# A two-layer attention, mLSTM and Mamba-2 encoder on one core: three token-stationary products at 512 columns, and a program order from an altered estimate

## The chip, the cores and the metric

The kernel runs on one core of one Trainium2 chip. The metric is device time in microseconds of one execution; before the change it is 1729.86 us (median of three runs, 1726.07 to 1732.43). The program is fixed: a Python layer writes out the instructions of every engine once, in one order, and the chip executes that order.

## The reference, cut to what matters

Two encoder layers run over 768 tokens of width 1024 (a request of 256 and one of 512), in float32. One layer is

```python
h = rms_norm(x, norm_g)
proj = h @ w_in                                   # 1024 -> 8224, all parts at once
ya = window_attention(rope(q), rope(k), v, sink) * silu(az)
yb = rms_norm(mlstm_bidir(mq, mk, mv, mi, mf)) * sigmoid(mo) * silu(mz)
yc = rms_norm(ssd_bidir(silu(conv(sxbc)), dt) * silu(sz))
merged = ga * (ya @ w_att_out) + gb * (yb @ w_mlstm_out) + gc * (yc @ w_ssm_out)
return x + merged @ w_out
```

where ga, gb and gc are sigmoids of further parts of proj.

## The kernel before, in words

**Products.** Every large product is computed in three parts: each float32 factor is split into a rounded high part and a remainder, both stored as float32r, and high*high, high*low and low*high are accumulated in PSUM. The activations lie split and transposed in the tile H. Weights come by DMA into a raw slot of 1024 words (`issue_raw`, line 591), ScalarE casts the high part, and VectorE or GpSimd subtracts it for the low part (`split_w`, 656). Split weights lie in one of four slots of 2048 words at the end of the tile R, or, for some pieces, in a block of R itself (`split_next`, 631).

**Items.** Each layer is a list of items (`ORDER`, line 20, built by `item_plan`). A "C" item (`item_C`, `mm_c`) keeps weights stationary and streams 512 and 256 tokens, so its output has channels on the partitions. A "T" item (`item_T`, 814, `mm_t`, 693) keeps 128 tokens stationary and streams the weights, so its output has tokens on the partitions: the queries (aq0, aq1), keys, values and gates (ak), the mLSTM values (mv0, mv1) and the SSD gate (sz0, sz1). aq, mv and sz are each two items of 256 columns. Per item and tile of 128 tokens that is 8 blocks of 128 rows times three parts, 24 matmuls. Weights of such an item are two pieces of 1024 words, dropped at the end of the item. "O", "P" and "W" items are the output products.

**Small work.** Norms, rotary embedding, attention, mLSTM and SSD are Python generators (`Task`, `Flow`, `mix_att`, `mix_mlstm`, `mix_ssd`, and the `..._put` functions behind each product). `tick` (557) is called between matmuls and writes the next steps of those generators whose inputs an estimate holds to be ready. `Clock.note` (238) keeps that estimate: when each engine is free and when each piece of memory was last written. `Watched.cost` (290) gives the duration of an instruction. The time "now" is the estimated time of TensorE. A transposition or a small matmul that a generator writes stands in TensorE's queue between the large matmuls; if its input is late on the chip, the large matmuls behind it wait too.

```python
t = max(t, (m[0][sl] + np.where(m[1][sl] != code, self.HOP, same)).max())
fin = t + cost
...
if ins[0].dtype == F32R:
    return max(53.0, n / 2.4)
```

All instructions are recorded through one helper, so the profile shows line 280 for each of them; they are told apart by tiles and shapes. "R,H" are the token-stationary products and the output product W, "H,R" the C items, "R" the products with the branch outputs, "F" the float32 transpositions and small matmuls.

**Memory.** The tile F holds 20096 words per partition, handed out and taken back by an `Arena` (102). Where there is no room, `alloc` raises an error while the program is written.

Of the kernel before, what the change touches and what calls it, by code (L numbers as in the profile page):

```python
# [55 lines left out]
def item_plan(layer):  # L56
# [4 lines left out]
    r0, r1, ra = range(0, 4), range(4, 8), range(0, 8)  # L61
# [15 lines left out]
    def one(word):  # L77
# [3 lines left out]
        elif name in ("aq", "mv", "sz"):  # L81
            t_item(name, idx, [({"aq": AQ, "mv": MV, "sz": SZ}[name] + 256 * idx, 256)])
# [101 lines left out]

INF = float("inf")


class Clock:
# [7 lines left out]
    def __init__(self):  # L196
        self.free = dict(pe=0.0, dve=0.0, act=0.0, pool=0.0, dma=0.0)
        self.mem = {}
        self.bank = [0.0] * 8
        self.psum = None  # L200
        self.last = 0.0

# [67 lines left out]
class Watched:  # L270
# [19 lines left out]
    def cost(self, name, out, ins, kw):  # L290
# [22 lines left out]
        if kw.get("op") == ALU.pow:  # L313
            return 300.0 + 164.0 * n
        return 150.0 + 2.1 * n
# [47 lines left out]
class Body:  # L363
    def __init__(self, tc, es, ins, outs):
# [44 lines left out]
        for l in range(NL):  # L409
            for kind, name, idx, pcs in item_plan(l):  # L410
# [10 lines left out]
                if name == "akv":  # L421
# [61 lines left out]
    def step(self, task, now):  # L483
# [11 lines left out]
        if isinstance(w, Task):  # L495
# [266 lines left out]
    def layer0_start(self):  # L762
# [16 lines left out]
        left = list(range(NT))  # L779
        for i in range(NT):  # L780
# [3 lines left out]
            if i < 2:  # L784
                self.issue_raw(1)
# [28 lines left out]
    def item_T(self, l, name, idx, ids):  # L814
# [10 lines left out]
        for i in ids:  # L825
            self.drop(i)

    def aq_begin(self, l, g):
        s = self.S[l]
        s["q", g] = self.R.alloc(4 * TOK)  # L830
        if g == 0:
            self.finish(s["consts"])
            s["k"] = self.R.alloc(4 * TOK)
            s["qkr"] = Ring(self.F, 5, 512)
            s["qks"] = Ring(self.F, 5, 8)

    def aq_epi(self, l, g, i, p):
        self.in_turn(self.S[l]["qkr"], lambda t: self.q_put(l, g, i, p, t))

    def qk_norm(self, l, i, p, nh, goff, t):  # L840
# [4 lines left out]
        t1, t2 = t[:, 0:n], t[:, 256:256 + n]  # L845
# [8 lines left out]
        self.rstd(st[:, 4:4 + nh], st[:, 0:nh], 1.0 / 64)  # L854
        yield
        nc.vector.tensor_tensor(out=a3, in0=a3, in1=st[:, 4:4 + nh].unsqueeze(2).to_broadcast([128, nh, 64]), op=ALU.mult)
# [12 lines left out]
    def q_put(self, l, g, i, p, t):  # L869
        nc = self.nc  # L870
        yield from self.qk_norm(l, i, p, 4, CB_QG, t)
        q4 = self.S[l]["q", g].ap.rearrange("p (j e t) -> p j e t", j=2, e=2)
        b, = yield 1
        for j in range(2):
            self.transpose_to(b[:, 128 * j:128 * j + 128], t[:, 128 * j:128 * j + 128])
        b3 = b[:, 0:256].rearrange("p (j t) -> p j t", j=2)
        ts = slice(128 * i, 128 * i + 128)
        half = [slice(0, 64), slice(64, 128)]
        for e in range(2):
            nc.scalar.copy(q4[half[e], :, e, ts], b3[half[e]])  # L880
        yield
        for e in range(2):
            nc.vector.tensor_tensor(out=q4[half[1 - e], :, e, ts], in0=b3[half[e]], in1=q4[half[e], :, e, ts].bitcast(F32),
                                    op=ALU.subtract)
        self.give(b)
        if i == NT - 1:
            self.flag(l, "qT", g)
# [15 lines left out]
    def k_put(self, l, i, p, t):  # L903
# [4 lines left out]
        nc.scalar.copy(t[:, 256:512].rearrange("p (v e d) -> p v e d", v=2, e=2),  # L908
                       t[:, 0:128].rearrange("p (v d) -> p v d", v=2).unsqueeze(2).to_broadcast([128, 2, 2, 64]))
        b, = yield 1  # L910
        for j in range(2):
            self.transpose_to(b[:, 128 * j:128 * j + 128], t[:, 256 + 128 * j:384 + 128 * j])
# [6 lines left out]
        if i == NT - 1:  # L919
            self.flag(l, "kT")  # L920

    def mv_begin(self, l, hp):
        s = self.S[l]
        b = s["mv", hp] = self.falloc(NT * 2 * 129)
        v = b.ap.rearrange("p (i h e) -> p i h e", i=NT, h=2)
        self.nc.gpsimd.memset(v[:, :, :, 128:129], 1.0)

    def mv_epi(self, l, hp, i, p):
        v = self.S[l]["mv", hp].ap.rearrange("p (i h e) -> p i h e", i=NT, h=2)
        self.nc.scalar.copy(v[:, i, :, 0:128], p.rearrange("p (h e) -> p h e", h=2))  # L930
        self.give(p)
        if i == NT - 1:
            self.flag(l, "mv", hp)

    def sz_begin(self, l, g):
        s, nc = self.S[l], self.nc
        if g == 0:
            s["szr"] = Ring(self.F, 3, 256)
            s["yc"] = self.R.alloc(8 * TOK)
            s["ycs"] = self.falloc(16)  # L940
            s["sng"] = self.falloc(512)
            s["ycr"] = Ring(self.F, 2, 512)
            s["ycn"] = NT

            def sng():
                nc.sync.dma_start(out=s["sng"].ap, in_=self.ins["cstb"][l:l + 1, CB_SNG:CB_ALL].to_broadcast([128, 512]))
                yield
                nc.gpsimd.tensor_scalar(out=s["sng"].ap, in0=s["sng"].ap, scalar1=0.5, scalar2=None, op0=ALU.mult)

            s["sngt"] = self.spawn(sng())  # L950
        else:
            self.finish(s["sngt"])
# [885 lines left out]
```

## Time and profile before

| | us |
|---|---|
| median of three runs | 1729.86 |
| the profiled execution | 1730.85 |
| its span | 1728.9 |
| TensorE busy | 1685.9 (98%) |
| VectorE busy | 938.6 (54%) |
| ScalarE busy | 643.5 (37%) |
| GpSimd busy | 382.8 (22%) |
| mean granted TensorE clock | 0.994 of full speed |

The span is from the first to the last instruction; the profiled execution took 1.95 us more than that. Busy times of matmuls overlap each other where they are pipelined, so durations of matmuls are best read from start to start.

### The profile page before, as it was taken

The page shows a single profiled execution, that of the slowest core. Times are in us where ns is not written, and L with a number is a line of the kernel's source. Part 1 is how long each engine was busy: PE and PEld are TensorE (multiplying, and loading weights), DVE is VectorE, ACT ScalarE, POOL GpSimd, SP SyncE. Part 2 cuts the span into 40 slices and gives each one's busy share as a digit, 9 for nine tenths or more (in the row PEclk, how much of TensorE's full clock was granted, in tenths as well). Part 3 has the DMA queues.
Part 4 walks back from the last instruction along what each step waited for, and adds up shares of the span by engine and source line. Part 5 has one row for each costly group of instructions (what it writes and reads, how often), then busy time and mean ns, then how long its engine had stood idle before and what let it go on. Part 6 is the DMA issues. An engine that isn't in the chain of part 4 may idle for free. (4 is left out here: it accounts for less than half of the span.)

```text
span 1728.9 us, 27389 instructions
## 1 busy us (share of the span) xinstructions
PE 1685.9 (98%) x10766; PEld 1487.3 (86%) x10766; DVE 938.6 (54%) x2176; ACT 643.5 (37%) x1461; POOL 382.8 (22%) x488
## 2 busy tenths in 40 slices
PE   8999999999999999999999999999999999999999
PEld 7888889988877878998798898898888878789987
DVE  6664556444577971256356544563445779613541
ACT  6446743322334421243143566432332244122320
POOL 6533310000113241014045333000001121400220
PEclk9999999999999999999999999999999999999999
DMA  4111122222114432145211101222121145222522
GB/s 175 63 50 38 38 95 77 79 77 71 57 51 140 168 111 90 56 155 168 97 62 39 62 25 50 83 77 89 67 71 59 61 147 189 99 75 68 183 85 74
DMA packets 47888, 152.29 MB, mean 88 GB/s; under 512 B 5616, under 2 KB 6544, under 8 KB 47760
## 3 DMA queue, kind: packets, MB, share of 16 engines
q1 hardware_dynamic: 47760, 150.55, 25.7%
q8 instruction: 85, 1.39, 0.3%
q14 instruction: 43, 0.35, 0.1%
HBM read 131.51 MB, written 19.02 MB: 87 GB/s over the span
## 5 line engine op out<-in xcount | busy, mean ns | idle before, releaser
L280 PE MATMUL psum<-H,R 128*128 128x512 f32 x4800 | 891.0, 341 | 0.1
L280 PEld LDWEIGHTS psum<-H,R 128*128 128x128 f32 x4800 | 734.9, 189 | 108.3 <-issue 8.9
L280 PE MATMUL psum<-R,H 128*128 128x256 f32 (+2 forms) x2616 | 397.5, 310 | 4.9 <-POOL R L280 3.1
L280 PEld LDWEIGHTS psum<-R,H 128*128 128x128 f32 x2616 | 360.4, 191 | 28.7 <-POOL R L280 3.3
L280 DVE TENSOR_TENSOR R<-F,R 128x1024 fp32r<-128x1024 f32 (+2 forms) x158 | 208.6, 1332 | 253.6 <-ACT R L280 253.5
L280 DVE SCALAR_TENSOR_TENSOR F<-F 128x128 f32<-128x128 f32 (+5 forms) x596 | 272.8, 504 | 59.8 <-POOL F L280 33.5
L280 PE MATMUL psum<-F 128*128 128x128 f32 (+7 forms) x2006 | 254.3, 289 | 34.9 <-DVE F L280 21.6
L280 POOL TENSOR_TENSOR F<-F 128x32 f32<-128x32 f32 (+8 forms) x276 | 226.9, 832 | 263.5 <-DVE F L280 222.8
L280 ACT ACTIVATE F<-F 128x128 f32<-128x128 f32 (+8 forms) x432 | 202.6, 496 | 185.8 <-DVE F L280 154.1
L280 PEld LDWEIGHTS psum<-F 128*128 128x128 f32 (+4 forms) x2006 | 203.0, 164 | 72.2 <-DVE F L280 29.5
L280 PE MATMUL psum<-R 128*128 128x512 f32 (+2 forms) x1344 | 249.8, 336 | 0.0
L280 ACT ACTIVATE F<-psum 128x768 f32<-128x768 f32 (+2 forms) x148 | 93.3, 630 | 397.0 <-PE psum L280 389.0
L280 POOL TENSOR_SCALAR F<-F 128x256 f32<-128x256 f32 (+7 forms) x124 | 78.8, 638 | 714.5 <-ACT F L280 521.3
L280 PEld LDWEIGHTS psum<-R 128*128 128x128 f32 x1344 | 204.3, 189 | 29.1 <-issue 3.0
L280 ACT CAST R<-F 128x1024 fp32r<-128x1024 f32 (+4 forms) x226 | 194.2, 876 | 70.5 <-DVE F L280 34.8
L280 ACT COPY F<-psum 128x256 f32<-128x256 f32 (+5 forms) x298 | 108.5, 392 | 207.6 <-PE psum L280 195.9
L280 DVE SCALAR_TENSOR_TENSOR F<-F,psum 128x768 f32<-128x768 f32 (+3 forms) x136 | 90.4, 674 | 109.6 <-ACT F L280 57.0
L280 POOL TENSOR_TENSOR R<-F,R 128x128 fp32r<-128x128 f32 (+2 forms) x68 | 76.3, 1124 | 246.0 <-ACT R L280 243.7
L280 DVE SCALAR_TENSOR_TENSOR F<-psum,F 128x128 f32<-128x128 f32 (+4 forms) x75 | 37.4, 505 | 161.1 <-PE psum L280 160.4
L280 DVE TENSOR_TENSOR F<-F 128x2 f32<-128x2 f32 (+8 forms) x376 | 102.6, 281 | 33.3 <-POOL F L280 16.5
L280 DVE TENSOR_SCALAR F<-F 128x128 f32<-128x128 f32 (+5 forms) x230 | 64.7, 309 | 49.7 <-ACT F L280 25.7
L280 DVE TENSOR_TENSOR F<-F,psum 128x129 f32<-128x129 f32 (+2 forms) x104 | 36.0, 376 | 39.2 <-ACT F L280 21.0
(24 smaller groups left out, 280.0 us busy)
## 6 DMA issues: line engine op xcount, KB each, us to landing
F<-wts_dram SPq DMA_DIRECT2D x164, 512.0 KB, 3.5
mg<-F SPq DMA_DIRECT2D x32, 384.0 KB, 3.0
F<-mg SPq DMA_DIRECT2D x32, 384.0 KB, 5.3
F<-csd SPq DMA_DIRECT2D x32, 384.0 KB, 5.7
F<-x_dram SPq DMA_DIRECT2D x12, 512.0 KB, 5.4
F<-md SPq DMA_DIRECT2D x16, 384.0 KB, 5.1
x<-F SPq DMA_DIRECT2D x6, 512.0 KB, 2.6
F<-x SPq DMA_DIRECT2D x6, 512.0 KB, 3.9
```

The source lines that it names most:

```text
L280: r = fn(*args, **kw)
```

## The change

aq, mv and sz become one item each per layer with 512 columns and four weight pieces of two row blocks (2 x 512 words). The functions behind them handle eight heads where there were four. For the last tile of a T item, `mm_t` goes through the pieces once and drops each as it has been used. The start of the kernel has two more raw slots, and asks for two pieces of weights behind each of the first two token tiles where it asked for one. In the estimate, an instruction of VectorE or GpSimd that reads two operands of over 8 elements from SBUF waits for the last such instruction of the other; a float32r matmul costs 13 ns plus its columns at 2.4 per ns; several other costs of TensorE and GpSimd are altered. Generators that need much memory ask for it (`Room`) and are not continued until it is there.

```diff
-aq0 ak0 az0 aq1 mo0 az1 az2 mk0 az3 mv0 mq0 mq1 mz0 mk1 oa0
-mo1 oa1 mz1 mv1 mq2 oa2 mk2 oa3 oa4 mo2 mq3 mk3 mz2 oa5 mo3
+aq0 ak0 az0 mo0 az1 az2 mk0 az3 mv0 mq0 mq1 mz0 mk1 oa0
+mo1 oa1 mz1 mq2 oa2 mk2 oa3 oa4 mo2 mq3 mk3 mz2 oa5 mo3
...
-ob6 ob7 gc0 gc1 gc2 gc3 gc4 gc5 sz0 sz1 gc6 gc7 oc0 oc1 oc2
+ob6 ob7 gc0 gc1 gc2 gc3 gc4 gc5 sz0 gc6 gc7 oc0 oc1 oc2
...
     def t_item(name, idx, cols):
-        plan.append(("T", name, idx, [("in", layer, r0, cols), ("in", layer, r1, cols)]))
+        plan.append(("T", name, idx, [("in", layer, range(2 * q, 2 * q + 2), cols) for q in range(4)]))
...
-            t_item(name, idx, [({"aq": AQ, "mv": MV, "sz": SZ}[name] + 256 * idx, 256)])
+            t_item(name, idx, [({"aq": AQ, "mv": MV, "sz": SZ}[name], 512)])
...
+class Room:
+    def there(self):
+        got = []
+        try:
+            for n in self.sizes:
+                got.append(self.arena.alloc(n))
+            return True
+        except MemoryError:
+            return False
+        finally:
+            for b in got:
+                b.free()
...
+    def two(self, ins):
+        n = 0
+        for ap in ins:
+            size = 1
+            for _, k in ap.ap[1:]:
+                size *= k
+            n += size > 8 and ap.tensor.name != self.psum
+        return n > 1
...
+        shared = eng in ("dve", "pool") and self.two(ins)
+        if shared:
+            t = max(t, self.port)
         fin = t + cost
+        if shared:
+            self.port = fin - 60.0
...
             if ins[0].dtype == F32R:
-                return max(53.0, n / 2.4)
+                return 13.0 + n / 2.4
             if out.offset // out.ap[0][0] == 64:
-                return 55.0
-            return max(107.0 * 2, n / 0.6)
+                return 12.0
+            return max(110.0 * 2, n / 0.6 + 6.0)
...
         if kw.get("op") == ALU.pow:
-            return 300.0 + 164.0 * n
-        return 150.0 + 2.1 * n
+            return 390.0 + 157.0 * n
+        if name == "tensor_scalar":
+            return 130.0 + 3.1 * n
+        return 130.0 + 2.2 * n
...
-                if name == "akv":
+                if name in ("akv", "sz"):
                     self.extra.update(ids)
...
+        if isinstance(w, Room):
+            if not w.there():
+                return False
...
     def mm_t(self, out, ids, i):
         j, tot = 0, 3 * sum(self.pieces[x][1] for x in ids)
+        if i == NT - 1:
+            self.finish(self.h_task[i])
+            k0 = 0
+            for x in ids:
+                whi, wlo = self.weights(x)
+                for k in range(self.pieces[x][1]):
+                    for w, a in ((whi, 0), (wlo, 0), (whi, 1)):
+                        self.nc.tensor.matmul(out=out, lhsT=self.hT(a, k0 + k, 128 * i, 128 * i + 128), rhs=w[:, k, :],
+                                              start=j == 0, stop=j == tot - 1)
+                        j += 1
+                    if k % 2:
+                        self.tick()
+                k0 += self.pieces[x][1]
+                self.drop(x)
+                self.tick()
+            return
...
+        self.more_raw(2)
         for i in range(NT):
...
             if i < 2:
-                self.issue_raw(1)
+                self.issue_raw(2)
...
+            s["qkr"] = Ring(self.F, 3, 1024)
+            s["qks"] = Ring(self.F, 3, 16)
...
-            s["szr"] = Ring(self.F, 3, 256)
+        s["szr"] = Ring(self.F, 3, 512)
...
+        yield Room(F, *[384] * 8, *[128] * 4, *[12] * 4)
```

**How the order of instructions moves.** Nearly every instruction stands at another place. First, TensorE from the first instruction on: "F" rows of 128x128 are transpositions (of normalised tokens, or of queries), "R,H" rows the query product aq. Before:

```order
L280 MATMUL psum<-F 128x128 x20
L280 MATMUL psum<-R,H 128x256 x12
L280 MATMUL psum<-F 128x128 x8
L280 MATMUL psum<-R,H 128x256 x18
L280 MATMUL psum<-F 128x128 x8
L280 MATMUL psum<-R,H 128x256 x18
L280 MATMUL psum<-F 128x128 x8
L280 MATMUL psum<-R,H 128x256 x42
```

and now:

```order
L316 MATMUL psum<-F 128x128 x20
L316 MATMUL psum<-R,H 128x512 x18
L316 MATMUL psum<-F 128x128 x8
L316 MATMUL psum<-R,H 128x512 x6
L316 MATMUL psum<-F 128x128 x8
L316 MATMUL psum<-R,H 128x512 x18
L316 MATMUL psum<-F 128x128 x16
L316 MATMUL psum<-R,H 128x512 x18
```

The first tile's 24 matmuls, of twice the columns, now stand nearly whole ahead of the second tile's transpositions, and need all four pieces of weights.

Second, VectorE where the convolution of the SSD branch begins in layer 0 (items sx4, sx5; `conv`, line 1062): one TENSOR_SCALAR and four SCALAR_TENSOR_TENSOR of 128x768 are the five taps, a fifth SCALAR_TENSOR_TENSOR ends the silu, and "R<-F,R 128x1024" is the low part of a weight piece. Before:

```order
L280 SCALAR_TENSOR_TENSOR F<-F,psum 128x768
L280 TENSOR_SCALAR F<-F 128x768
L280 SCALAR_TENSOR_TENSOR F<-F 128x768 x5
L280 TENSOR_SCALAR F<-F 128x768
L280 SCALAR_TENSOR_TENSOR F<-F 128x768 x2
L280 TENSOR_TENSOR R<-F,R 128x1024
L280 SCALAR_TENSOR_TENSOR F<-F 128x768 x3
```

and now:

```order
L316 SCALAR_TENSOR_TENSOR F<-F,psum 128x768
L316 TENSOR_SCALAR F<-F 128x768
L316 TENSOR_TENSOR R<-F,R 128x1024
L316 SCALAR_TENSOR_TENSOR F<-F 128x768 x5
L316 TENSOR_SCALAR F<-F 128x768
L316 TENSOR_TENSOR R<-F,R 128x1024
L316 SCALAR_TENSOR_TENSOR F<-F 128x768 x5
```

Each convolution now has a weight split of its own behind the first tap; before, every second one had.

Third, GpSimd over the same stretch and on to the end of the SSD branch (128x512: state inputs and outputs; 128x768: sums of the output products). Before:

```order
L280 MEMSET F 128x4
L280 MEMSET F 128x2
L280 TENSOR_TENSOR R<-F,R 128x1024 x4
L280 TENSOR_TENSOR F<-F 128x512 x8
L280 TENSOR_TENSOR F<-F 128x768
L280 TENSOR_TENSOR R<-F,R 128x1024
L280 TENSOR_TENSOR F<-F 128x768 x3
```

and now:

```order
L316 MEMSET F 128x4
L316 MEMSET F 128x2
L316 TENSOR_TENSOR F<-F 128x512 x3
L316 TENSOR_TENSOR R<-F,R 128x1024
L316 TENSOR_TENSOR F<-F 128x512 x5
L316 TENSOR_TENSOR F<-F 128x768 x7
L316 TENSOR_TENSOR F<-F 128x512 x8
```

The four splits that stood on GpSimd during the convolutions are gone from there.

## Rows read from the trace of the kernel before

**Rows 1.** Spans and clock; then busy time by engine, from the page.

```profile
core 0: 1728.9 us, clock 0.994
PE 1685.9 (98%) x10766; PEld 1487.3 (86%) x10766; DVE 938.6 (54%) x2176; ACT 643.5 (37%) x1461; POOL 382.8 (22%) x488
```

**Rows 2.** What TensorE waited for most: total us, times, longest us.

```profile
PE psum L280 <- DVE F L280: 22.1, 21, 3.2
```

**Rows 3.** TensorE's timeline, items gc and sz of layer 0 (start, duration).

```profile
666.42 50.08 PE L280 MATMUL psum<-H,R 128*128 128x512 f32 x288
716.34 26.07 PE L280 MATMUL psum<-R,H 128*128 128x256 f32 x216
742.24 0.60 PE L280 MATMUL psum<-F 128*128 128x128 f32 x4
742.60 1.68 PE L280 MATMUL psum<-R,H 128*128 128x256 f32 x12
744.12 0.60 PE L280 MATMUL psum<-F 128*128 128x128 f32 x4
```

**Rows 4.** TensorE's timeline, convolutions: first and last of eight waits (in brackets).

```profile
478.97 0.87 PE L280 MATMUL psum<-F 128*128 128x128 f32 x6 [1.16 <-DVE F L280]
...
1386.54 0.88 PE L280 MATMUL psum<-F 128*128 128x128 f32 x6 [0.53 <-DVE F L280]
```

**Rows 5.** VectorE's timeline in the convolutions of layer 0.

```profile
480.16 2.07 DVE L280 SCALAR_TENSOR_TENSOR F<-F 128x768 f32<-128x768 f32 x2
482.15 1.22 DVE L280 TENSOR_TENSOR R<-F,R 128x1024 fp32r<-128x1024 f32 x1
...
489.40 6.26 DVE L280 SCALAR_TENSOR_TENSOR F<-F 128x768 f32<-128x768 f32 x4
```

**Rows 6.** GpSimd's timeline in the same stretch.

```profile
489.29 2.40 POOL L280 TENSOR_TENSOR R<-F,R 128x1024 fp32r<-128x1024 f32 x1 [16.29 <-ACT R L280]
```

**Rows 7.** TensorE's timeline, SSD heads: from the first to the last of ten waits.

```profile
570.45 1.55 PE L280 MATMUL psum<-F 128*128 128x64 f32 x12 [0.43 <-DVE F L280]
...
578.04 1.55 PE L280 MATMUL psum<-F 128*128 128x64 f32 x12 [1.81 <-DVE F L280]
...
625.05 2.82 PE L280 MATMUL psum<-F 128*128 128x64 f32 x12 [1.01 <-DVE F L280]
...
1481.98 1.55 PE L280 MATMUL psum<-F 128*128 128x64 f32 x12 [1.01 <-DVE F L280]
```

**Rows 8.** Stretches: length; PE, PEld, DVE, ACT, POOL busy; clock, DMA, GB/s.

```profile
580.00:600.00 20.00, 20.00 (x117) 17.73 (x116) 18.61 (x48) 8.84 (x18) 1.90 (x1) 0.92 0.35 116
620.00:640.00 20.00, 17.79 (x92) 13.45 (x92) 12.44 (x30) 1.75 (x2) 7.87 (x7) 0.83 0.05 20
1440.00:1460.00 20.00, 20.00 (x125) 17.82 (x124) 19.93 (x47) 11.66 (x24) 3.36 (x2) 1.00 0.46 158
```

**Rows 9.** TensorE's timeline, transpositions of queries and keys: first and last of ten waits.

```profile
44.72 0.44 PE L280 MATMUL psum<-F 128*128 128x128 f32 x2 [1.24 <-POOL F L280]
...
962.77 0.44 PE L280 MATMUL psum<-F 128*128 128x128 f32 x2 [0.73 <-POOL F L280]
```

**Rows 10.** GpSimd's timeline, query norms and rotary embedding.

```profile
81.47 1.26 POOL L280 TENSOR_TENSOR F<-F 128x32 f32<-128x32 f32 x4 [1.65 <-DVE F L280]
...
83.10 1.02 POOL L280 TENSOR_TENSOR F<-F 128x4 f32<-128x4 f32 x1
...
96.31 3.07 POOL L280 TENSOR_TENSOR F<-F 128x32 f32<-128x32 f32 x4 [1.91 <-DVE F L280]
```

**Rows 11.** The start: TensorE's wait, ScalarE's cast, GpSimd's split, and one stretch.

```profile
15.96 1.01 PE L280 MATMUL psum<-R,H 128*128 128x256 f32 x3 [3.12 <-POOL R L280]
11.36 1.05 ACT L280 CAST R<-F 128x1024 fp32r<-128x1024 f32 x1
12.49 3.42 POOL L280 TENSOR_TENSOR R<-F,R 128x1024 fp32r<-128x1024 f32 x1
14.00:16.00 2.00, 0.04 (x1) 0.04 (x1) 0.00 (x0) 0.00 (x0) 2.00 (x2) 0.50 1.02 417
```

More of the change, by code (lines that the diff above doesn't have):

```diff
@@ L201, in __init__ @@
         self.last = 0.0
+        self.port = 0.0
     def add(self, ap, psum=False):
@@ L824, in item_T, with aq_begin, aq_epi, qk_done @@
             epi(l, idx, i, p)
-        for i in ids:
-            self.drop(i)
-    def aq_begin(self, l, g):
+        if l == 0 and name == "aq":
+            self.more_raw(0)
+    def aq_begin(self, l, _):
         s = self.S[l]
[L830 to L838, printed above, removed]
+        self.finish(s["consts"])
+        for g in range(2):
+            s["q", g] = self.R.alloc(4 * TOK)
+        s["k"] = self.R.alloc(4 * TOK)
+        s["qkr"] = Ring(self.F, 3, 1024)
+        s["qks"] = Ring(self.F, 3, 16)
+        s["qkn"] = 2 * NT
+    def aq_epi(self, l, _, i, p):
+        self.in_turn(self.S[l]["qkr"], lambda t: self.q_put(l, i, p, t))
+    def qk_done(self, l):
+        s = self.S[l]
+        s["qkn"] -= 1
+        if s["qkn"] == 0:
+            for k in ("qkr", "qks"):
+                s.pop(k).free()
     def qk_norm(self, l, i, p, nh, goff, t):
@@ L867, in qk_norm, with q_put @@
         gp.tensor_tensor(out=a3[:, :, 0:16], in0=a3[:, :, 0:16], in1=b3[:, :, 0:16], op=ALU.add)
[L869 removed]
+    def q_put(self, l, i, p, t):
         nc = self.nc
[L871 to L872 removed]
+        yield from self.qk_norm(l, i, p, 8, CB_QG, t)
         b, = yield 1
[L874 removed]
+        for j in range(4):
             self.transpose_to(b[:, 128 * j:128 * j + 128], t[:, 128 * j:128 * j + 128])
[L876 removed]
         ts = slice(128 * i, 128 * i + 128)
         half = [slice(0, 64), slice(64, 128)]
[L879 to L880 removed]
+        parts = [(self.S[l]["q", g].ap.rearrange("p (j e t) -> p j e t", j=2, e=2),
+                  b[:, 256 * g:256 * g + 256].rearrange("p (j t) -> p j t", j=2)) for g in range(2)]
+        for q4, b3 in parts:
+            for e in range(2):
+                nc.scalar.copy(q4[half[e], :, e, ts], b3[half[e]])
         yield
[L882 to L884 removed]
+        for q4, b3 in parts:
+            for e in range(2):
+                nc.vector.tensor_tensor(out=q4[half[1 - e], :, e, ts], in0=b3[half[e]], in1=q4[half[e], :, e, ts].bitcast(F32),
+                                        op=ALU.subtract)
         self.give(b)
         if i == NT - 1:
[L887 removed]
+            self.flag(l, "qT", 0)
+            self.flag(l, "qT", 1)
+        self.qk_done(l)
     def akv_begin(self, l, _):
@@ L920, in k_put, with mv_begin @@
             self.flag(l, "kT")
-    def mv_begin(self, l, hp):
+        self.qk_done(l)
+    def mv_begin(self, l, _):
         s = self.S[l]
[L924 to L930, printed above, removed]
+        for hp in range(2):
+            b = s["mv", hp] = self.falloc(NT * 2 * 129)
+            v = b.ap.rearrange("p (i h e) -> p i h e", i=NT, h=2)
+            self.nc.gpsimd.memset(v[:, :, :, 128:129], 1.0)
@@ L931, in mv_epi, with sz_begin @@
+    def mv_epi(self, l, _, i, p):
+        for hp in range(2):
+            v = self.S[l]["mv", hp].ap.rearrange("p (i h e) -> p i h e", i=NT, h=2)
+            self.nc.scalar.copy(v[:, i, :, 0:128], p[:, 256 * hp:256 * hp + 256].rearrange("p (h e) -> p h e", h=2))
         self.give(p)
         if i == NT - 1:
-            self.flag(l, "mv", hp)
-    def sz_begin(self, l, g):
+            self.flag(l, "mv", 0)
+            self.flag(l, "mv", 1)
+    def sz_begin(self, l, _):
         s, nc = self.S[l], self.nc
-        if g == 0:
-            s["szr"] = Ring(self.F, 3, 256)
[L939 to L952, printed above, removed]
@@ L1304, in mix_gates @@
         s, nc, F = self.S[l], self.nc, self.F
+        yield Room(F, *[144] * 3, 720, 48, *[272] * 5, 192, 48, 128)
         v, sc = nc.vector, nc.scalar
@@ L1503, in mix_att @@
         if g == 1:
-            for k in ("pr", "ar", "as", "k", "v", "qkr", "qks"):
+            for k in ("pr", "ar", "as", "k", "v"):
                 s.pop(k).free()
@@ L1519, in mix_mlstm @@
         if h == 0:
+            yield Room(F, 1536, 1536, TOK, 1032, *[129] * 3, *[258] * 3, *[4] * 3, 12, 12)
             s["mb"] = Ring(F, 2, 1536)
@@ L1642, in mix_mlstm @@
         self.give(b)
-        yield
+        yield Room(self.R, 2 * TOK)
         y = s["yb", h] = self.R.alloc(2 * TOK)
@@ L1663, in mix_ssd @@
         Bc, Cc = s["sx", 4].ap, s["sx", 5].ap
+        yield Room(F, 2048, 512, 512, 512)
         stb = F.alloc(8 * 256)
@@ L1694, in mix_ssd @@
         s.pop("BT").free()
+        yield Room(F, *[TOK] * 8)
         lr = Ring(F, 6, TOK)
@@ L1751, in mix_ssd @@
         cbb.free()
+        yield Room(F, 512, 512)
         orr = Ring(F, 2, 512)
```

44 lines of the change are left out of this document (26 added, 18 removed).

## The prediction

> **What bounds the kernel now.** I read the list of spans, the clock and the busy times first: TensorE is busy for 1685.9 of 1728.9 us, the next engine, VectorE, for 938.6 [rows 1]. So time can be saved in two ways only: less work on TensorE, or fewer of the 43.0 us in which it stands. The second view is what TensorE waited for [rows 2]: of its 22.1 us behind VectorE no wait is longer than 3.2 us, so this is a sum of many small ones. The timeline of TensorE then gives the price of its work and the places of the waits. I sorted them: eight at the convolutions, 7.8 us [rows 4]; ten at the SSD heads, 9.3 us [rows 7]; ten at the transpositions of queries and keys, 10.1 us [rows 9]; the rest lies at the start, at the layer boundary and at the end.
>
> The sum below is made against the profiled execution, 1730.85 us, which is 1.0 us above the median of the runs and inside their spread of 6.4 us. A measurement of this kernel can tell a difference of about 0.5% (8.6 us) from no change.
>
> **1. The columns: -11.3 us.** From start to start, 216 matmuls of 256 columns take 742.24 - 716.34 = 25.90 us, 119.9 ns each [rows 3]. The 288 matmuls ahead of them are 144 pairs of 512 and 256 columns in 716.34 - 666.42 = 49.92 us, 346.7 ns a pair, which leaves 226.8 ns for one of 512 [rows 3]. Two matmuls of 256 cost 239.8 ns, so each pair made one saves 13.0 ns. aq, mv and sz are six items of 144 matmuls in each of two layers, 1728 of 256 columns; they become 864 of 512, and 864 x 13.0 = 11.3 us. All of it is on TensorE, the bound, so it comes off the end. The Trainium skill speaks against this: by "TensorE: Matmul & The Clock Gate", section "Wait — 56ns, not 53.3ns?", a warm matmul costs its columns at 2.4 GHz and about 2.5 ns more, so that the saving would be an estimated 864 x 2.5 = 2.2 us. The rows of this float32r kernel have a fixed part of about 13 ns in both kinds of stretch, and I go by them.
>
> **2. Fewer changes between large and small matmuls: -1.6 us.** A run of 12 matmuls between transpositions takes 744.12 - 742.60 = 1.52 us against 12 x 119.9 = 1.44 [rows 3], so 0.08 us per interruption. I counted 257 runs of float32 work in TensorE's order before and 237 now: 20 x 0.08. With no such price it is 0.
>
> **3. The convolutions: -5.8 us.** Tap instructions take 1.04 us each (two in 2.07) [rows 5], but four took 6.26 where GpSimd ran a weight split of 2.40 us at the same time [rows 5, 6]: one of them was held for 6.26 - 4 x 1.04 = 2.1 us. In the new order these splits are on VectorE, behind the first tap, at 1.22 us [rows 5]. The chain to the transposition is thus 2.1 - 1.22 = 0.9 us shorter. The transpositions also move: counted in pairs of matmuls from the first sx item, the five of a layer stand 2 pairs later, 2 later, 2 earlier, 2 later and 4 earlier (0.35 us a pair). The waits of 1.16, 1.16 and 1.07 us a layer fall to about nothing; the last, 0.53, grows to about 1.0. That leaves 1.0 of 3.9 us in each layer. Bounds: 0 if something else is late in the same chain, -7.8 if all eight go.
>
> **4. The heads: -6.5 us, and -3.4 us of clock.** Between the first and last of a layer's head products TensorE's order held 128 pairs, 44.4 us, of large work; on the chip that took 625.05 - 570.45 = 54.6 us [rows 7], and VectorE was busy for 93% and 99% of two such stretches [rows 8], so VectorE set the pace. Now the order holds 170 pairs, 58.9 us, in between. With 7 head products of 1.3 us, that gives VectorE 68 us for what took it 54.6. I keep 1.4 us of waits a layer for unevenness and for the first head, which stands 4 pairs sooner, and take 6.5 of the 9.3 us. Bounds: 0 and -9.3. The granted clock fell there in layer 0 alone, behind waits of 1.81 and 1.01 us among others [rows 7]: means of 0.92 and 0.83 over two stretches of 20 us, against 1.00 in layer 1 [rows 8]. The mean stands for a mixture of the 1.2 and 2.4 GHz levels; what is lost is 20 x (0.08 + 0.17) = 5.0 us of full-speed work. If the waits go, most of it should; I take 3.4, the share of the second stretch. Bounds: +3 (layer 1 falls too) and -5.
>
> **5. Queries and keys: -5 us.** The ten waits are on GpSimd and ScalarE [rows 9]. A tile's query norm and rotary embedding cost GpSimd 1.02 + 1.26 us for four heads, the second piece 3.07 where VectorE got in between [rows 10]. For eight heads I double it: 4.6 us, against 24 x 0.227 = 5.4 us of TensorE work per tile, so GpSimd just keeps up. There are half as many transposition groups, and they are written later. I take half of the 10.1 us. Bounds: -10, and +5 if GpSimd falls behind. The Trainium skill has a rule that the new estimate follows only in part: by "SBUF — State Buffer", section "SBUF: two separate sides", any GpSimd instruction, and a VectorE one with two SBUF inputs, take the shared ports for the whole instruction. The estimate counts instructions with two inputs of over 8 elements alone, so pow over 8 columns and one-input steps stay outside it. By the rule these waits stay; that is a rival below.
>
> **6. The start: 0.** TensorE waited 3.12 us for a split on GpSimd [rows 11], and the clock was at its 1.2 GHz level there [rows 11]. Now the first tile needs four pieces instead of two, and one more split of 3.42 us on GpSimd; but while later tiles are normalised, there is twice the work. On SP's queue the second to fourth pieces pass ahead of tokens: the third tile's tokens land two pieces later. ScalarE casts two more pieces (1.05 us each) ahead of the second and third tiles' norms. I set these against each other. Bounds: -3 and +4, one GpSimd split each way.
>
> **7. Weight slots: +3 us.** A 512-column item fills all four slots. The next item's first piece can be split only when the last tile has dropped one: 18 matmuls, 4.1 us, before the end. Cast and VectorE split take 1.05 + 1.22 = 2.3 us [rows 5, 11], so this fits unless other work is queued ahead; with GpSimd it is 4.5 and does not. Six items (aq, mv, sz, twice): nearest is the VectorE row, and I allow 0.5 us each. Bounds 0 and +12 (2 us each). The splits for sz may use blocks of R.
>
> Room costs no instruction. Its cover is the slack of the mixers: layer 0's last head product stood at 625 us [rows 7], sz began at 716 [rows 3]; the new order still has the whole of gc, 50 us [rows 3], in between. Without that cover TensorE would stand until the mixer ends. Wider ScalarE and VectorE work lies on engines under 55% and costs nothing while they have this room; if they lose it, transpositions are late next.
>
> Sum: -11.3 - 1.6 - 5.8 - 6.5 - 3.4 - 5 + 0 + 3 = -30.6, so 1730.85 - 30.6 = **1700 us**, 1.7% less.
>
> **The rivals.**
> *Only the columns pay (13%).* The estimate is better but the chip finds other late inputs: a matmul of 256 was taken as 106.7 ns and really takes 119.9, so the old order had hidden slack for the small work, and the new one has it no more. For it: waits of 7 to 10 us came at all three kinds of place. Against: steps 3 and 4 rest on counts in the order, not on the estimate. Time: 1730.85 - 11.3 = 1719.5.
> *The port is still in the way for queries (10%).* Step 5 gives nothing: 1705.
> *The 13 ns grow with the columns (3%).* Then a matmul of 512 costs 2 x 119.9 = 239.8 ns, step 1 gives nothing, and with the waits as they are the time is 1731. Against: the 144 pairs of step 1. By the page named there it would be 1730.85 - 2.2 = 1728.6.
> *Slots starve TensorE (4%), slower.* If each of the six items waits at both ends for a cast and a GpSimd split, 4.5 us, that is 12 x 4.5 = 54 us, less the 30.6 - (-3) = 33.6 of the other steps: 1751. It decides from 33.6 / 12 = 2.8 us per wait; to be measurably slower it needs 3.5. For it: all four slots are taken. Against: pieces are dropped one by one, and in the order GpSimd has 15 splits of 1024 words, 17 before.
> That the change does less than it says is seen only in the estimate; the matmuls are halved in the order itself.
>
> **How the numbers follow.** The forecast has 70%, with 1686 to 1714 as its own range (steps 3 to 5 at half or whole, step 7 at 0 to 12). The second rival lies inside it. Reaching up to the columns-only time takes in half of that rival: 1686 to 1720 leaves out about 6% (columns only, a little worse), 3%, 4% and some 5% below. Faster by over 0.5% means under 1721.2: 70 + 10 and 9 of the 13 are 89%; the same: 4 + 3 and a share of small slot losses, 8%; slower: 3%.
>
> **What would show it.** The by-shape list: 1416 matmuls of 512 columns in "R,H", 48 of 256, start to start 227 ns. TensorE busy near 1670 us and idle near 28. At the convolutions no wait over 0.5 us but the last; GpSimd without splits there; no taps of 3 us. At the heads waits under 1.5 us a layer and a clock of 1.00. In the wait list VectorE under 10 us. Wrong, if TensorE's idle time is still 40 us or more, if large matmuls wait for ScalarE's casts or splits at the ends of aq, mv and sz, or if a 512-column matmul takes 240 ns.

## The result and the profile after

The changed kernel takes **1718.91 us** (median of nine runs, 1714.10 to 1724.93), against 1729.99 (nine runs, 1725.14 to 1735.20) for the kernel before: a ratio of 0.9940, 95% interval 0.9922 to 0.9959. It is faster, but by 11 us where 30.6 were forecast; the time lies inside the range, near its upper end. The profiled execution took 1719.23 us. First the span and the busy times on its page, which answer to [rows 1], then the list of cores:

```profile
span 1717.4 us, 25480 instructions
PE 1678.1 (98%) x9902; PEld 1440.5 (84%) x9902; DVE 916.6 (53%) x2121; ACT 642.7 (37%) x1425; POOL 333.5 (19%) x411
```

```profile
core 0: 1717.4 us, clock 0.994
```

TensorE's busy time fell by 7.8 us. Its idle time went from 43.0 to 1717.4 - 1678.1 = 39.3 us, where 28 had been forecast. The next view is what TensorE waited for: us in total, times, longest. It answers to [rows 2].

```profile
PE psum L316 <- POOL F L316: 16.5, 10, 3.6
PE psum L316 <- DVE F L316: 7.1, 10, 1.5
PE psum L316 <- DVE R L316: 5.3, 8, 1.9
```

In the kernel before, the row behind GpSimd was

```profile
PE psum L280 <- POOL F L280: 7.2, 7, 1.5
```

The waits behind VectorE fell from 22.1 to 7.1 us, as the forecast had it. But those behind GpSimd more than doubled, to 16.5. Sorted by place, TensorE's waits were and are:

| place | before | forecast | after |
|---|---|---|---|
| convolutions | 7.8 | 2.0 | 0.0 |
| SSD heads | 9.3 | 2.8 | 3.9 |
| queries and keys | 10.1 | 5.1 | **17.9** |
| start, before 26 us | 8.3 | 8.3 | 7.0 |
| slots of the weights | 0 | 3 | 1.2 |
| rest | 3.7 | 3.7 | 5.7 |
| sum | 39.3 | 25.0 | 35.7 |

(The rows are rounded. The other 3.6 to 3.7 us of idle time are not put down to a wait.) In the rest, a wait of 3.21 us at the layer boundary fell to 0.35, and two of 1.91 us came at the output products.

At queries and keys one period of the repeating pattern is this, in the timeline of after (start, us, engine, operation; in brackets the idle time before it and what ended it):

```profile
43.93 0.66 PE L316 MATMUL psum<-F 128*128 128x128 f32 x4 [1.12 <-POOL F L316]
43.96 0.20 POOL L316 TENSOR_SCALAR F<-F 128x8 f32<-128x8 f32 x1
44.24 1.64 POOL L316 TENSOR_TENSOR F<-F 128x8 f32<-128x8 f32 x1
44.34 5.71 PE L316 MATMUL psum<-R,H 128*128 128x512 f32 x24
44.62 1.50 ACT L316 CAST R<-psum 64x256 fp32r<-64x256 f32 x4 [4.66 <-PE psum L316]
46.15 1.73 DVE L316 TENSOR_TENSOR R<-psum,R 64x256 fp32r<-64x256 f32 x4 [3.48 <-ACT R L316]
47.91 1.42 DVE L316 TENSOR_TENSOR F<-F 128x512 f32<-128x512 f32 x2
49.48 1.65 POOL L316 TENSOR_TENSOR F<-F 128x64 f32<-128x64 f32 x4 [3.60 <-DVE F L316]
51.19 0.66 PE L316 MATMUL psum<-F 128*128 128x128 f32 x4 [1.14 <-POOL F L316]
```

From one transposition to the next are 51.19 - 43.93 = 7.26 us, of which TensorE works for 7.26 - 1.14 = 6.12. Each step waits for the one above it: ScalarE casts the transposed tile i, VectorE subtracts it, and only behind that, in the same queue, come the multiplies of tile i+1, though the pow that they need ended at 44.24 + 1.64 = 45.88. GpSimd's rotary embedding needs the multiplies, and the next transposition needs the embedding. From start to start the steps are 0.69 + 1.53 + 1.76 + 1.57 + 1.71 = 7.26 us. GpSimd is busy for 0.20 + 1.64 + 1.65 = 3.5 us of it: it is not too slow, it is idle for half the time, and VectorE, with 1.73 + 1.42 us in these rows, is idle for about as long. My theory (A in what follows) is that this **loop through in-order queues**, which only the 512-column tiles close, ate what the columns gave.

### The profile page after: what moved, and what is told of

Its sections match the earlier page's. It is cut to its first block, busy times and chain, and to the rows that moved or that the text cites. A ratio compares the mean times of both kernels' runs of the same rounds, so it can differ in the third digit from the quotient of the medians.

```text
span 1717.4 us, 25480 instructions
## 1 busy us (share of the span) xinstructions
PE 1678.1 (98%) x9902; PEld 1440.5 (84%) x9902; DVE 916.6 (53%) x2121; ACT 642.7 (37%) x1425; POOL 333.5 (19%) x411
## 4 chain that ended last, share of the span: by engine, by line
PE 87%; DVE 6%; ACT 2%; POOL 2%; DMA 1%; issue 1%; SPq 0%; ACTq 0%; POOLq 0%; DVEq 0%
PE psum L316 87%; DVE F L316 3%; DVE R L316 2%; POOL F L316 2%; ACT R L316 1%; ACT F L316 1%; DMA F<-wts_dram 1%; DMA F<-csd 1%; DMA F<-cstb_dram 0%; POOL R L316 0%; SPq L316 0%; DVE H L316 0%; ACT H L316 0%; ACTq L316 0%; POOLq L316 0%
## 5 line engine op out<-in xcount | busy, mean ns | idle before, releaser
L316 PE MATMUL psum<-R,H 128*128 128x512 f32 (+2 forms) x1752 | 392.2, 379 | 8.1 <-DVE R L316 4.8
L316 PEld LDWEIGHTS psum<-R,H 128*128 128x128 f32 x1752 | 310.7, 191 | 66.0 <-DVE R L316 7.4
L316 DVE TENSOR_TENSOR R<-F,R 128x1024 fp32r<-128x1024 f32 (+3 forms) x163 | 206.6, 1278 | 243.6 <-ACT R L316 242.0
L316 POOL TENSOR_TENSOR F<-F 128x32 f32<-128x32 f32 (+9 forms) x216 | 202.4, 946 | 441.7 <-DVE F L316 243.2
L316 PE MATMUL psum<-F 128*128 128x128 f32 (+5 forms) x2006 | 247.7, 287 | 27.4 <-POOL F L316 16.5
L316 PEld LDWEIGHTS psum<-F 128*128 128x128 f32 (+2 forms) x2006 | 202.3, 163 | 67.3 <-POOL F L316 21.2
L316 ACT CAST R<-F 128x1024 fp32r<-128x1024 f32 (+3 forms) x226 | 195.0, 875 | 100.7 <-DVE F L316 50.9
L316 PEld LDWEIGHTS psum<-R 128*128 128x128 f32 x1344 | 204.2, 189 | 30.6 <-issue 2.1
L316 ACT COPY F<-psum 128x256 f32<-128x256 f32 (+7 forms) x286 | 105.2, 402 | 175.9 <-PE psum L316 174.4
L316 POOL TENSOR_TENSOR R<-F,R 128x128 fp32r<-128x128 f32 (+1 forms) x63 | 60.1, 957 | 318.2 <-ACT R L316 294.0
L316 DVE TENSOR_SCALAR F<-F 128x128 f32<-128x128 f32 (+5 forms) x230 | 67.4, 322 | 45.9 <-ACT F L316 22.1
L316 DVE TENSOR_TENSOR R<-psum,R 64x256 fp32r<-64x256 f32 (+2 forms) x72 | 33.5, 466 | 47.6 <-ACT R L316 46.8
```

The lines of the kernel that those rows point to most:

```text
L316: r = fn(*args, **kw)
```

## The experiments

### The two parts of the change apart

The estimate alone (the code of `Clock`, `Watched` and `Room` as in the change, 256 columns), and the columns alone (the change with these costs as before):

```diff
-                return max(53.0, n / 2.4)
+                return 13.0 + n / 2.4
...
+        if shared:
+            t = max(t, self.port)
```

> The kernel before with the altered estimate and Room alone; the columns stay at 256. Theory A (the estimate pays at the convolutions and heads, the 512-column queries cost what it brings): the waits at the convolutions fall from 7.8 to under 1 us, at the heads from 9.3 to about 4, those at queries and keys stay near 10; 1716 to 1722 us. Theory B (only the columns paid, the waits just moved): 1727 to 1732 us, idle time of TensorE still 43 us.

> The changed kernel with the estimate of before; 512 columns and Room stay. Theory A: convolution and head waits are back at 7.8 and 9.3 us, the waits at queries and keys at about 18 us; 1726 to 1731 us, hardly under the kernel before. Theory B: 1717 to 1721 us, as the changed kernel.

Measured: the estimate alone 1721.08 us, ratio 0.9943 (0.9923 to 0.9963), as theory A had it; the columns alone 1735.18, ratio 1.0027 (1.0012 to 1.0043), some 4 us above A's highest and far from B. From the list of waits, first of the estimate alone, then of the columns alone:

```profile
PE psum L316 <- DVE F L316: 12.1, 14, 1.5
PE psum L316 <- POOL F L316: 5.3, 6, 2.0
```

```profile
PE psum L299 <- DVE F L299: 22.1, 24, 2.9
PE psum L299 <- POOL F L299: 17.7, 11, 3.7
```

Each part moves its own row. The estimate cuts the VectorE row (at the convolutions nothing is left, at the heads 4.7 us) and leaves queries and keys at about 10 us. The columns leave the VectorE row at the 22.1 of before and raise the GpSimd row from 7.2 to 17.7; queries and keys wait 17.9 us, just as in the changed kernel. So the gain came with the estimate. The columns, which I had priced at -11.3, gave nothing on their own: what they saved in TensorE's work went into waits (46.8 us in all against 39.3) and into the clock (13.4 us against 10.2, in the table at the end).

### The loop opened

One edit on the changed kernel: a tile's subtracts are written only once the next tile's multiplies are.

```diff
     def qk_norm(self, l, i, p, nh, goff, t):
...
+        if nh == 8:
+            self.flag(l, "qm", i)
...
     def q_put(self, l, i, p, t):
...
-        yield
+        yield (l, "qm", i + 1) if i + 1 < NT else None
```

> The changed kernel; VectorE now multiplies the next query tile by its norm ahead of subtracting the low part of the previous one, by an order held in the generators. The transpositions stand at the same places in TensorE's queue or up to 6 matmuls earlier. Theory A (the 17.9 us of query waits are a loop from one transposition to the next through ScalarE, VectorE's subtraction, VectorE's multiplication and GpSimd, 7.26 us a tile against 5.9 of TensorE work): the loop loses 1.7 us, the waits between query tiles fall from 1.1 to 2.2 us each to under 0.4, in total by 6 to 12 us; 1705 to 1713 us. Theory C (the transpositions simply stand too early for GpSimd's port): waits as before or longer, 1717 to 1722 us.

Measured: **1710.25 us**, ratio 0.9880 (0.9864 to 0.9896); waits at queries and keys 9.8 us. The same tile in this kernel's timeline:

```profile
43.33 1.50 ACT L316 CAST R<-psum 64x256 fp32r<-64x256 f32 x4 [2.17 <-PE psum L316]
43.59 1.64 POOL L316 TENSOR_TENSOR F<-F 128x8 f32<-128x8 f32 x1
45.26 1.42 DVE L316 TENSOR_TENSOR F<-F 128x512 f32<-128x512 f32 x2 [2.04 <-POOL F L316]
46.71 1.73 DVE L316 TENSOR_TENSOR R<-psum,R 64x256 fp32r<-64x256 f32 x4
46.82 1.69 POOL L316 TENSOR_TENSOR F<-F 128x64 f32<-128x64 f32 x4 [1.59 <-DVE F L316]
48.62 0.60 PE L316 MATMUL psum<-F 128*128 128x128 f32 x4
```

The multiplies now wait for the pow alone, and the transposition at 48.62 us has no wait. Nothing was made cheaper; two groups in one queue changed places, for 8.7 us against the changed kernel.

### Transpositions later, and the wrong group first

The opposite order held fast from the third tile on, with the transpositions planned 1.5 us later:

```diff
-        yield
+        yield (l, "qs", i - 1) if nh == 8 and i >= 2 else None
...
+        self.clk.last += 1500.0
         b, = yield 1
...
+        self.flag(l, "qs", i)
```

> The changed kernel with the query transpositions written 1.5 us later by the estimate (6 matmuls and more), and VectorE held to subtracting the previous tile before multiplying the next. Theory A (loop): each tile still needs 7.2 us, the waits between query tiles stay at 1 us or more, total within 4 us of 17.9; 1715 to 1721 us. Theory C (too early): waits fall to under 6 us in all; 1704 to 1710 us.

Measured: 1724.17 us, ratio 0.9963 (0.9949 to 0.9976), above the 1715 to 1721 of theory A; the waits, 19.4 us, were as A had them. The time that is too long is the clock's: at full clock (the table at the end) this kernel takes 1708.3 us, the changed one 1709.2. Placing the consumer later does not help when its producer is tied to the consumer before it; the later place with a free order was not tried. The longest wait of this kernel:

```profile
70.20 1.11 PE L316 MATMUL psum<-F 128*128 128x128 f32 x4 [5.22 <-POOL F L316]
```

### The queries alone back at 256 columns

```diff
-aq0 ak0 az0 mo0 az1 ...
+aq0 ak0 az0 aq1 mo0 az1 ...
...
-        elif name in ("aq", "mv", "sz"):
-            t_item(name, idx, [({"aq": AQ, "mv": MV, "sz": SZ}[name], 512)])
+        elif name == "aq":
+            plan.append(("T", name, idx, [("in", layer, r, [(AQ + 256 * idx, 256)]) for r in (range(0, 4), range(4, 8))]))
+        elif name in ("mv", "sz"):
+            t_item(name, idx, [({"mv": MV, "sz": SZ}[name], 512)])
```

The functions behind aq handle four heads again, with five buffers.

> The kernel after with the queries alone as two items of 256 columns again (five buffers of 512 words); mv and sz stay at 512. Theory A (the 512-column query tiles form a loop through the in-order queues; the columns of mv and sz pay as counted): TensorE's waits at queries and keys fall from 17.9 us to 8 to 12, the 256-column matmuls cost 288 x 13 ns = 3.7 us more, 1712 to 1717 us. Rival B (the width of the query tiles is harmless, the new places of the transpositions are what costs): the waits stay at 15 us or more, 1720 to 1725. Rival C (512 columns pay nothing in mv and sz either): waits of 8 to 12 but a time like that of the new estimate alone, 1719 to 1723.

Measured: 1711.42 us, ratio 0.9887 (0.9872 to 0.9902), a little under theory A's 1712 to 1717; waits at queries and keys 6.6 us, under A's 8 to 12. The kernel has 288 matmuls more than the changed one and is 7.5 us faster. From its waits:

```profile
PE psum L318 <- POOL F L318: 4.5, 5, 1.8
```

So, of the three wide products, the queries lost mostly by their order and not by their width as such, and narrowing them or reordering them mends the same loss.

### The heads later, alone and on top

The products of the SSD heads planned 1.5 us later, in the changed kernel and in the one with the loop opened:

```diff
     def head(h):
...
+            self.clk.last += 1500.0
             b, = yield 1
```

> The kernel after with the products of the SSD heads planned 1.5 us later; nothing else is edited. The second head's product moves 4 large matmuls later against the first, and the fourth 40 later. Theory A (the granted clock falls at 600 to 640 us because of the one 1.53 us wait there): the waits at the heads go from 3.9 us to 1 or less and the clock stays at 1.00, which gives 3 us of waits and 3.4 of clock, 1711 to 1714 us. Rival B (the clock falls for another reason): only the waits go, 1715 to 1717. Rival C (the heads that are planned later make later ones late): waits of 4 us or more, 1718 to 1722.

> Both edits together: the next tile's multiplies ahead of the subtracts, and the heads' products planned 1.5 us later. Theory A: the two gains lie in different stages and add up, 1710.25 - (5 to 7) = 1703 to 1705 us. Rival B (only the waits at the heads go): 1706 to 1709. Rival C (the heads' edit gives nothing): 1709 to 1712.

Measured: 1717.35 us, ratio 0.9918 (0.9903 to 0.9933), and with the loop opened 1705.55, ratio 0.9852 (0.9837 to 0.9866). The first misses theory A's 1711 to 1714; it is 1.6 us under the changed kernel, which these runs cannot tell from none. The second misses its 1703 to 1705 by half a microsecond, and is clear of the loop opened alone. Two rows of 20 us each (stretch, its length, then busy us of TensorE, its weight loads, VectorE, ScalarE and GpSimd; granted clock, DMA share, GB/s), of after and then of the kernel with the heads later:

```profile
600.00:620.00 20.00, 18.47 (x101) 16.50 (x101) 15.65 (x40) 8.04 (x18) 1.88 (x1) 0.86 0.46 150
620.00:640.00 20.00, 20.00 (x121) 17.81 (x120) 13.43 (x31) 8.65 (x14) 2.74 (x1) 0.97 0.28 93
```

```profile
600.00:620.00 20.00, 20.00 (x130) 18.00 (x129) 19.87 (x52) 9.27 (x21) 4.28 (x2) 1.00 0.54 182
620.00:640.00 20.00, 18.66 (x116) 15.83 (x114) 14.53 (x27) 7.04 (x12) 2.31 (x2) 1.00 0.41 138
```

The clock stays at 1.00 there, as A said. But the waits at the heads only fell from 3.9 to 3.2 us (A: 1 or less), and what the clock gave here it took elsewhere: over all runs, the time lost to it (span times one minus the mean clock) is 9.9 us against 10.3. At full clock (the table at the end) the edit is worth about 1.9 us in either kernel, hardly more than four runs can show.

### GpSimd's splits out of VectorE's way

With the loop opened one long wait was left at queries and keys. The timeline of the kernel with both edits shows GpSimd, VectorE and TensorE around it:

```profile
908.39 2.37 POOL L316 TENSOR_TENSOR R<-F,R 128x1024 fp32r<-128x1024 f32 x1 [0.95 <-ACT R L316]
```

```profile
908.43 2.88 DVE L316 TENSOR_TENSOR F<-F 128x512 f32<-128x512 f32 x1
```

```profile
913.87 1.11 PE L316 MATMUL psum<-F 128*128 128x128 f32 x4 [3.86 <-POOL F L316]
```

A multiply of 0.71 us (two took 1.42) takes 2.88 beside a GpSimd weight split of 2.37: it ends at 911.31 us, just behind the split's end at 910.76. On top of both edits, one kernel sends the splits to VectorE while queries and keys are made, a second also those of the output product (`wide`, handed to `split_w`); the line of the second:

```diff
-        g = self.nc.vector if at["dve"] <= at["pool"] else self.nc.gpsimd
+        g = self.nc.vector if at["dve"] <= at["pool"] + (4000.0 if wide or any("qkr" in s for s in self.S) else 0.0) else self.nc.gpsimd
```

> As the run with both edits, and while queries and keys are made weight splits go to VectorE (two splits of the second layer move, 576 and 1024 words). Theory A (the 3.70 us wait at 917.86 us is VectorE's multiplies held to 4.00 us by a GpSimd split of 2.81 us): that wait falls to 1.5 us or less, 2 to 4 us under the run with both edits. Rival B (the wait comes from the queue's order, not from the split): it stays over 3 us and the time is within 1 us of that run.

> The kernel of the run without splits on GpSimd (1701.3 us), and in each layer one more weight split, the one of the output product at 791.34 us, moves from GpSimd to VectorE; TensorE's order is the same. There VectorE's second split seems to wait until GpSimd's split ends at 794.70 us and ends 1.2 us later, which is when TensorE goes on after 1.91 us. Theory A (the two engines take turns on two-input instructions): without it VectorE's second split ends about 2 us sooner, both waits of 1.91 us fall under 0.3, three splits that took 7.34 us take under 5.5, and the time is 1696 to 1699 us. Rival B (the splits were late because of the casts or of VectorE's own queue): the waits stay over 1.2 us, 1700 to 1703 us.

Measured: 1701.27 us, ratio 0.9831 (0.9815 to 0.9848), 4.3 us under the kernel with both edits where A had 2 to 4, and with the output product's splits **1695.91**, ratio 0.9801 (0.9778 to 0.9823), the fastest of this study and faster than both kernels. First the place of the long wait in the former, then the output product in the latter:

```profile
904.14 1.42 DVE L316 TENSOR_TENSOR F<-F 128x512 f32<-128x512 f32 x2 [0.36 <-POOL F L316]
...
908.32 0.66 PE L316 MATMUL psum<-F 128*128 128x128 f32 x4 [0.91 <-POOL F L316]
```

```profile
788.78 11.53 PE L316 MATMUL psum<-R,H 128*128 128x512 f32 x50
...
790.72 6.28 DVE L316 TENSOR_TENSOR R<-F,R 128x1024 fp32r<-128x1024 f32 x4
```

In the changed kernel the second of these places read:

```profile
798.79 7.34 DVE L316 TENSOR_TENSOR R<-F,R 128x1024 fp32r<-128x1024 f32 x3
800.55 3.36 POOL L316 TENSOR_TENSOR R<-F,R 128x1024 fp32r<-128x1024 f32 x1
...
805.05 4.37 PE L316 MATMUL psum<-R,H 128*128 128x512 f32 x11 [1.91 <-DVE R L316]
```

The second kernel came out at the lower edge of A's 1696 to 1699. VectorE does four splits alone in less time than three beside one of GpSimd's, and TensorE's wait of 1.91 us is gone in both layers. TensorE's order of instructions is the same in the last two kernels; only one split a layer changed its engine.

### The narrow queries with the same help

The queries at 256 columns with the heads' edit and no split on GpSimd at queries and keys, to see whether the width pays once the loop is open.

> Queries as two items of 256 columns, heads planned 1.5 us later, no weight split on GpSimd while queries and keys are made: the counterpart of the fastest run so far (1701.3 us), which has 512-column queries with the multiplies ahead of the subtracts. Theory A (512 columns are worth their 3.7 us for the queries too, once the loop through the queues is undone): 1703 to 1707 us. Rival B (the smaller tiles wait so much less that the width gives nothing): 1698 to 1702 us, with under 4 us of waits at queries and keys.

Measured: 1704.54 us, ratio 0.9858 (0.9835 to 0.9882): theory A's time, though the waits, 4.9 us, are not far above the 4 that rival B wanted. The counterpart with wide queries is 3.3 us faster, about the 3.7 that 288 x 13 ns give. The two kernels' runs overlap (1699.97 to 1703.73 and 1702.52 to 1706.84), so this difference alone is not clear of noise; at full clock it is 3.1 us, and between the narrow queries and the opened loop, both without the other edits, 4.2. The wide product is worth having, for two tenths of a per cent, once the order around it is right.

## Why the prediction was wrong

Against the sum of -30.6, the profiled executions differ by 1719.23 - 1730.85 = -11.6 us. The time is within 1 us of the 1719.5 of the rival *only the columns pay*, but that is chance: by the two kernels with one part each, it was the estimate that paid. Step by step:

**Steps 1 and 2, columns and interruptions: -12.9 forecast, about -8 measured.** The price of a matmul is as forecast. In the by-shape list, then in TensorE's timeline of sz:

```profile
L316 PE MATMUL psum<-R,H 128*128 128x512 f32 x1416 | 343.6, 398 | 7.6 <-DVE R L316 4.8 <-POOL R L316 2.4 <-ACT H L316 0.3
```

```profile
710.47 11.11 PE L316 MATMUL psum<-R,H 128*128 128x512 f32 x48
721.41 0.60 PE L316 MATMUL psum<-F 128*128 128x128 f32 x4
```

From start to start these 48 take 721.41 - 710.47 = 10.94 us, 227.9 ns each, so a pair of 256 made one saves 239.8 - 227.9 = 11.9 ns: 864 x 11.9 = 10.3 us. Busy time less what the clock took (one minus the granted clock, summed over the span) went from 1685.9 - 10.2 to 1678.1 - 10.4, which is -8.0. By the same sum the eight profiled kernels with 9902 matmuls lie between 1665.8 and 1669.5 us, the two with 10766 at 1675.6 and 1676.0: 6 to 10 us apart. Nothing in the runs shows a gain from fewer interruptions, and what took the other 2 us of step 1 stays open. The rival by which the 13 ns grow with the columns is out. So is the small saving that I had from the Trainium skill ("TensorE: Matmul & The Clock Gate", section "Wait — 56ns, not 53.3ns?"): its fixed part of about 2.5 ns a matmul would be an estimated 2.2 us, and these rows have 227.9 - 512/2.4 = 14.6 ns.

**Step 3, the convolutions: -5.8 forecast, -7.8 measured.** Right in its mechanism. The splits are on VectorE there, and the taps take 4.18 / 4 = 1.05 us each:

```profile
489.89 1.22 DVE L316 TENSOR_TENSOR R<-F,R 128x1024 fp32r<-128x1024 f32 x1
491.02 4.18 DVE L316 SCALAR_TENSOR_TENSOR F<-F 128x768 f32<-128x768 f32 x4
```

No tap is held any more, as four were for 6.26 us in [rows 5]. I had let the last wait of a layer grow to 1 us; it went too.

**Step 4, the heads: -6.5 forecast, -5.4 measured; the clock: -3.4 forecast, +0.2 in the profiled pair.** The waits shrank nearly as counted; what is left stands at the first head and where the products of two heads follow closely. But behind the one wait of 1.53 us in layer 0 the clock fell to 0.86 and 0.97 in two rows of 20 us, 20 x (0.14 + 0.03) = 3.4 us against 5.0 before, and it fell in two other rows where it had not before (those from 60 and 1640 us). That part of the step was wrong: I let the clock's loss shrink with the sum of the waits there, and one wait can be enough.

```profile
564.97 1.55 PE L316 MATMUL psum<-F 128*128 128x64 f32 x12 [0.99 <-DVE F L316]
614.35 2.72 PE L316 MATMUL psum<-F 128*128 128x64 f32 x12 [1.53 <-DVE F L316]
```

**Step 5, queries and keys: -5 forecast, +7.8 measured. This is the step that failed**, by 12.8 us of the 19 missing (columns and interruptions miss 4.9, the clock 3.6, waits that were not forecast about 2, the heads' waits 1.1; steps 3, 6 and 7 gave about 5 more than forecast). "For eight heads I double it: 4.6 us, against 24 x 0.227 = 5.4 us of TensorE work per tile, so GpSimd just keeps up." That compares throughputs. The doubled work was even less than I said (3.5 us), and still TensorE waited, because the way from one transposition to the next goes through four queues, and most instructions in it got about twice as long while the number of tiles in flight shrank from five of four heads to three of eight. I had named +5 "if GpSimd falls behind" as the bound; it did not fall behind. The bound was too small and its reason was the wrong one. The opened loop, the narrow queries and the tightened order together (9.8, 6.6 and 19.4 us of waits against 17.9) show the loop; that the number of buffers had a part in it was not tried.

The rival that the port stays in the way for queries holds a part of the truth. Around the third tile of the changed kernel:

```profile
56.73 2.75 POOL L316 TENSOR_TENSOR F<-F 128x64 f32<-128x64 f32 x4 [3.60 <-DVE F L316]
57.10 4.60 DVE L316 TENSOR_TENSOR R<-F,R 128x864 fp32r<-128x864 f32 x4
59.54 0.66 PE L316 MATMUL psum<-F 128*128 128x128 f32 x4 [2.23 <-POOL F L316]
59.57 1.06 POOL L316 TENSOR_SCALAR F<-F 128x8 f32<-128x8 f32 x1
60.71 2.49 POOL L316 TENSOR_TENSOR F<-F 128x8 f32<-128x8 f32 x1
61.77 1.73 DVE L316 TENSOR_TENSOR R<-psum,R 64x256 fp32r<-64x256 f32 x4
```

Beside VectorE's weight splits, GpSimd's rotary embedding takes 2.75 us, not the 1.65 of the tile shown first, and TensorE waits 2.23 us, not 1.14. GpSimd's two instructions of 8 columns take 1.06 and 2.49 us, not 0.20 and 1.64. The new estimate leaves these two out (one has a single input, neither is over 8 elements). Here that cost nothing: they end at 60.71 + 2.49 = 63.20 us, and VectorE's subtracts hold the multiplies until 63.50. With the loop opened the same instructions do hold the multiplies:

```profile
58.26 1.42 DVE L316 TENSOR_TENSOR F<-F 128x512 f32<-128x512 f32 x2 [0.39 <-POOL F L316]
```

The Trainium skill's rule ("SBUF — State Buffer", section "SBUF: two separate sides"), that a GpSimd instruction reading SBUF and a VectorE one with two inputs in SBUF take the shared ports in turn, each for its whole length, agrees with these rows, and the limits of the estimate do not. How much of the 17.9 us is the port's was not tried by itself.

**Step 6, the start: 0 forecast, -1.3 measured**, inside its bounds. **Step 7, the slots: +3 forecast, +1.2 measured**: five waits of 0.17 to 0.41 us; the splits kept up. The rival in which slots starve TensorE is out.

Not in the forecast at all: the two waits of 1.91 us at the output products, which came because the splits there met GpSimd's in the new order.

## What to carry to other kernels

When a tile grows, lay out the whole way from one use of the bottleneck to the next, queue by queue, and compare its length with the bottleneck's work per tile; that each engine has time enough says little. In such a loop, look in every in-order queue for an instruction of the next tile that stands behind one of this tile and could go first. And where two engines take turns on memory, moving work to the engine with more idle time can make both late: four splits on VectorE ended sooner than three there and one on GpSimd.

## What was not expected of the hardware

The granted clock does not follow from the program alone, nor from the length of a wait. The same wait of 1.91 us at the output products stands twice in each of nine profiles (the changed kernel, and the experiments except the columns alone and the last kernel, in which it is gone), and in 8 of these 18 cases the clock fell within 2 us of its end; in the others it did not. At the heads the clock fell within 2 us of the end of all eight waits of 1.52 to 1.55 us, and of only one of four waits of 1.73 to 1.81 us (in the kernel before and the columns alone). First TensorE's timeline and the row of 20 us in after, then in the kernel without splits on GpSimd:

```profile
1652.00 8.23 PE L316 MATMUL psum<-R,H 128*128 128x512 f32 x28 [1.91 <-DVE R L316]
```

```profile
1640.00:1660.00 20.00, 18.09 (x78) 14.68 (x77) 13.10 (x11) 5.37 (x6) 8.31 (x3) 0.91 0.22 80
```

```profile
1634.34 5.98 PE L316 MATMUL psum<-R,H 128*128 128x512 f32 x25 [1.91 <-DVE R L316]
```

```profile
1640.00:1660.00 20.00, 20.00 (x90) 16.57 (x89) 1.80 (x3) 0.00 (x0) 0.00 (x0) 1.00 0.33 106
```

A row of 0.91 is a mixture of the 1.2 and 2.4 GHz levels and costs 20 x 0.09 = 1.8 us, as much again as the wait before it. Runs of one and the same program differ by this: the columns alone took 1728.58 us at a mean clock of 0.996 and 1740.82 at 0.989, a difference of 12.2 us where 0.007 of its span is 12.1. Means over the runs, taken apart by each run's own clock and span (the clock is recorded to 0.001, which is 1.7 us; those of before are the runs beside the experiments):

| kernel | runs | mean us | at full clock | lost to the clock |
|---|---|---|---|---|
| before | 39 | 1730.7 | 1720.4 | 10.2 |
| estimate alone | 4 | 1721.0 | 1711.6 | 9.5 |
| columns alone | 10 | 1735.0 | 1721.6 | 13.4 |
| the change | 9 | 1719.6 | 1709.2 | 10.3 |
| loop opened | 4 | 1710.1 | 1700.3 | 9.8 |
| wrong group first | 5 | 1724.1 | 1708.3 | 15.8 |
| queries at 256 columns | 4 | 1711.8 | 1704.5 | 7.3 |
| heads later | 4 | 1717.1 | 1707.3 | 9.9 |
| loop opened, heads later | 4 | 1705.6 | 1698.4 | 7.2 |
| and no split on GpSimd there | 4 | 1701.6 | 1697.7 | 3.8 |
| and none at the output product | 6 | 1695.9 | 1692.6 | 3.4 |
| queries at 256 columns, heads later, no such split | 4 | 1704.6 | 1700.8 | 3.8 |

At full clock the columns with the new estimate give 1709.2 - 1711.6 = -2.4 us, with the old one 1721.6 - 1720.4 = +1.2. Of the 4.0 us that the run without splits on GpSimd gained, 3.4 are clock; that this comes from the one wait of 3.86 us is likely, but with means over four runs not shown. What decides whether the clock falls after a given wait stays open. The Trainium skill ("TensorE: Matmul & The Clock Gate", section "What's actually happening") calls it run-variable how many matmuls at the start of a kernel run at the lower level. No run here shows that by itself; over whole runs, the ten of the columns alone have mean clocks from 0.989 to 0.996.
